# A list scheduler's other timing model in a one-core decoder trunk

## The chip, the cores and the metric

The program runs on one NeuronCore of a Trainium2 chip. The metric is the device time of one execution in microseconds (us). PE is TensorE, DVE is VectorE, ACT is ScalarE, POOL is GpSimd, SP is SyncE; SPq is SP's queue of transfers.

## The reference

One inference step of a two-layer decoder for two groups that share weights: 1024 prompt tokens and 8 x 4 sample tokens, width 1024, float32.

```python
for layer in range(DEPTH):                      # 2: layer 0 pooling, layer 1 attention
    u = _rmsnorm(x, g[0])
    if layer < N_A_LAYERS:
        mix = _pool_mix(u, buf, start_pos, w_pool[layer], pool_scale[layer])
    else:
        kv = _rmsnorm(x, kv_norm_gain) @ w_kv   # rotated keys, values, shared
        mix = _dilated_mixer(u, pos, k_all, v_all, cache_k.shape[1], w_q[b], w_o[b])
    x = x + _rmsnorm(mix, g[1])
    h = _rmsnorm(x, g[2])
    ff = jnp.square(jax.nn.relu(h @ w_up[layer])) @ w_down[layer]
    x = x + _rmsnorm(ff, g[3])
```

The pooling mixer takes trailing means over 2, 4, 8 and 16 positions per channel group, minus the token, through a 256 x 256 matrix each. The attention has three groups of windows (128, 512, 2048) with dilations 1, 4 and 16, 18 query heads and 6 key/value heads, joined by the softmax of their denominators. The sample tokens also read cached keys and values.

## The kernel before

Tokens are split into two halves: half 0 holds 512 prompt tokens and the 32 sample tokens (544 columns, worked on as two pieces of 272), half 1 holds the other 512. Activations lie with channels on partitions. Every large product is done in three passes so that float32 precision is kept with the faster number format: each operand is split into a high and a low part, and `mm3` (lines 76 to 78) multiplies high by high, high by low and low by high into one PSUM tile.

Weights stream from memory: `load_w` (line 93) fetches 128 x 1024 values into one of two `raw` buffers on SP's queue, ACT copies the high part (`wh`, line 82) and DVE subtracts to get the low part (`wl`, line 83). There are 300 such loads. The MLP goes through its 4096 hidden channels in eight chunks: up products, squared ReLU on ACT (lines 368 and 369), a split of the result, and down products added to `y` on DVE (line 383).

The stages follow one another like this: the pooling mixer of half 0 and the first chunk of its MLP; the mixer of half 1; the other chunks of the MLP of half 0; its tail beside the MLP of half 1; projections, attention blocks and the joining of half 0, with the MLP of half 1 beside them; the tail of that MLP (lines 483 to 486 are the residual) and the projections of half 1 (lines 554, 563, 600 to 625), with the output projection of half 0 and its MLP in layer 1 beside them; attention of half 1; its output projection; the last MLPs and the end.

Two things set the order of the work. The first is the program order: generators yield the time that their matmuls are thought to take, and `drive` weaves a main stream and a stream beside it by these figures and by the gaps that the main stream announces. The second is a list scheduler, which runs when the `with tile.TileContext(...)` block closes. It plays the program through a timing model of the engines, and whenever an engine is free in that model it takes, of the instructions whose operands the model says are ready, the one that stands first. What stands first is program order, except that `tc.high_priority()` moves work forward: without limit inside `first()`, by 300 places in `load_w`. The queue that each engine gets in this way is fixed in the program: on the chip an engine's instructions are issued in that order, and each waits for its semaphores. Which of a pool's buffers a tile gets is settled in the same pass.

## Time and profile before

| | us |
|---|---|
| median of 3 runs | 2099.57 |
| lowest and highest | 2098.55, 2101.83 |
| profiled execution, its own time | 2098.92 |
| span of its trace | 2097.1 |
| PE busy in it | 2000.3 |
| DVE, ACT, POOL busy | 1211.7, 932.6, 147.5 |

The span runs from the first to the last instruction of the trace; the execution's time has 1.8 us around it. Busy time of PE is that of its matmuls, which overlap, and the ends of matmuls are modelled; weight loads (PEld) overlap them.

### The profile page before, as it was taken

What the parts mean: (1) busy time and instruction counts of PE and PEld (TensorE: products, weight loads), DVE (VectorE), ACT (ScalarE), POOL (GpSimd) and SP (SyncE); (2) the same over time, 40 slices, a digit from 0 to 9 for tenths busy, and PEclk for the clock granted to TensorE, in tenths of its full rate; (3) what the DMA queues carried; (4) which work ended last, traced back from release to release, by engine and by line L of the source; (5) the groups of instructions that cost most, each with busy time, mean ns of one, the idle gap of its engine ahead of it and who ended that gap; (6) DMA issues with size and microseconds to landing.
All of it is one profiled execution on the core that took longest, in us unless ns stands there. A gap on an engine that the chain in (4) does not pass through costs nothing. (4 is left out here: it accounts for less than half of the span.)

```text
span 2097.1 us, 30907 instructions
## 1 busy us (share of the span) xinstructions
PE 2000.3 (95%) x12161; PEld 1767.9 (84%) x12161; DVE 1211.7 (58%) x2044; ACT 932.6 (44%) x1730; POOL 147.5 (7%) x146
## 2 busy tenths in 40 slices
PE   5889999999999999999998889999999999999996
PEld 4859999998889877677796779999999897888886
DVE  6668443447766665454688746555564387444446
ACT  4536333335344365353554425555553364333333
POOL 1000000000322000000014200000000003000001
PEclk8999999999999999999999999999999999999998
DMA  9213323224455654533536565452232364323331
GB/s 176 94 33 126 94 84 91 88 84 134 142 152 162 177 175 123 178 102 110 175 121 200 154 173 168 128 143 90 91 116 91 95 210 165 107 92 98 93 100 61
DMA packets 127506, 262.07 MB, mean 125 GB/s; under 512 B 34560, under 2 KB 60032, under 8 KB 126336
## 3 DMA queue, kind: packets, MB, share of 16 engines
q1 hardware_dynamic: 117504, 242.30, 39.4%
q10 hardware_dynamic: 8736, 10.78, 1.6%
q0 software_dynamic: 1120, 7.00, 1.0%
q8 instruction: 96, 1.57, 0.3%
q14 instruction: 50, 0.41, 0.1%
HBM read 218.49 MB, written 41.55 MB: 124 GB/s over the span
## 5 line engine op out<-in xcount | busy, mean ns | idle before, releaser
L76 PE MATMUL mm<-xh,wh 128*128 128x272 f32 (+1 forms) x2088 | 679.3, 327 | 21.7 <-ACT xh L345 7.0
L78 PE MATMUL mm<-xh,wl 128*128 128x272 f32 (+1 forms) x2088 | 678.4, 325 | 1.3 <-DVE wl L83 1.3
L77 PE MATMUL mm<-xl,wh 128*128 128x272 f32 (+1 forms) x2088 | 676.5, 324 | 0.7 <-DVE xl L969 0.7
L82 ACT ACTIVATE wh<-raw 128x1024 fp32r<-128x1024 f32 x300 | 317.7, 1059 | 672.8 <-PE mm L77 585.4
L83 DVE TENSOR_TENSOR wl<-raw,wh 128x1024 fp32r<-128x1024 f32 x300 | 371.9, 1240 | 331.6 <-ACT wh L82 319.6
L76 PE MATMUL mm<-h,wh 128*128 128x272 f32 (+1 forms) x1504 | 485.3, 325 | 4.4 <-ACT wh L82 2.9
L77 PE MATMUL mm<-h,wh 128*128 128x272 f32 (+1 forms) x1504 | 483.8, 323 | 1.9 <-DVE h L83 1.8
L78 PE MATMUL mm<-h,wl 128*128 128x272 f32 (+1 forms) x1504 | 481.7, 322 | 2.2 <-DVE wl L83 2.2
L76 PEld LDWEIGHTS mm<-xh,wh 128*128 128x128 f32 x2088 | 394.7, 190 | 55.8 <-ACT xh L345 7.5
L78 PEld LDWEIGHTS mm<-xh,wl 128*128 128x128 f32 x2088 | 395.6, 190 | 31.3 <-DVE wl L83 1.9
L77 PEld LDWEIGHTS mm<-xl,wh 128*128 128x128 f32 x2088 | 396.0, 190 | 30.0 <-DVE xl L969 1.2
L76 PEld LDWEIGHTS mm<-h,wh 128*128 128x128 f32 x1504 | 282.0, 188 | 31.5 <-ACT h L82 6.8
L77 PEld LDWEIGHTS mm<-h,wh 128*128 128x128 f32 x1504 | 283.6, 189 | 24.9 <-DVE h L83 5.6
L383 DVE TENSOR_TENSOR y<-mm,y 128x272 f32<-128x272 f32 (+2 forms) x344 | 176.7, 514 | 219.7 <-PE mm L78 218.9
L78 PEld LDWEIGHTS mm<-h,wl 128*128 128x128 f32 x1504 | 282.7, 188 | 22.6 <-DVE wl L83 2.9
L83 DVE TENSOR_TENSOR h<-r,h 128x272 fp32r<-128x272 f32 (+1 forms) x192 | 102.8, 538 | 104.6 <-ACT h L82 104.0
L368 ACT ACTIVATE r<-mm 128x272 f32<-128x272 f32 (+1 forms) x192 | 86.3, 452 | 75.1 <-PE mm L78 73.8
L743 ACT ACTIVATE P<-P,nm 128x256 f32<-128x256 f32 (+1 forms) x144 | 66.0, 459 | 73.8 <-DVE nm L741 66.1
L82 ACT ACTIVATE h<-r 128x272 fp32r<-128x272 f32 (+1 forms) x192 | 94.6, 496 | 6.0 <-DVE br L605 1.7
L369 ACT ACTIVATE r<-r 128x272 f32<-128x272 f32 (+1 forms) x192 | 94.6, 496 | 4.7 <-ACT r L368 0.3
L97 POOL TENSOR_TENSOR raw<-raw,gn 128x768 f32<-128x768 f32 (+2 forms) x54 | 77.3, 1448 | 154.9 <-DMA raw<-in_wqkv 108.9
L166 ACT ACTIVATE t<-y 128x544 f32<-128x544 f32 (+2 forms) x75 | 44.5, 606 | 40.0 <-DVE y L383 31.3
(249 smaller groups left out, 1625.0 us busy)
## 6 DMA issues: line engine op xcount, KB each, us to landing
raw<-in_wmlp SPq DMA_DIRECT2D x256, 512.0 KB, 3.5
raw<-in_wqkv SPq DMA_DIRECT2D x30, 512.0 KB, 3.9
raw<-in_wo SPq DMA_DIRECT2D x18, 512.0 KB, 3.5
xh<-kd SPq DMA_DIRECT2D x12, 512.0 KB, 10.5
qd<-P SPq DMA_DIRECT2D x72, 64.0 KB, 2.6
xh<-qd SPq DMA_DIRECT2D x6, 768.0 KB, 5.7
oscr<-og ACTq DMA_DIRECT2D x24, 192.0 KB, 4.0
kv<-in_vc SPq DMA_DIRECT2D x18, 256.0 KB, 4.4
```

The lines of the kernel that those rows point to most:

```text
L76: nc.tensor.matmul(out=ps, lhsT=w[0][:, c], rhs=a, start=first, stop=False)
L77: nc.tensor.matmul(out=ps, lhsT=w[0][:, c], rhs=b, start=False, stop=False)
L78: nc.tensor.matmul(out=ps, lhsT=w[1][:, c], rhs=a, start=False, stop=last)
L82: nc.scalar.activation(out=hi, in_=src, func=AF.Copy)
L83: (eng or nc.vector).tensor_tensor(out=lo, in0=src, in1=wf(hi), op=OP.subtract)
L97: nc.gpsimd.tensor_tensor(out=v, in0=v, in1=self.gn[:, g * 8:g * 8 + 8].unsqueeze(2).to_broadcast([128, 8, c1 - c0]), op=OP.mult)
L166: nc.scalar.activation(out=s, in_=src, func=AF.Square, scale=scale)
L368: nc.scalar.activation(out=r, in_=ps, func=AF.Relu)
L369: nc.scalar.activation(out=r, in_=r, func=AF.Square)
L383: nc.vector.tensor_tensor(out=ys, in0=ps, in1=ys, op=OP.add)
L743: nc.scalar.activation(out=P[:, r, z:], in_=P[:, r, z:], func=AF.Exp, bias=nm[:, r:r + 1], scale=SCL, accum_out=st[:, b, 1, kv * 3 + r:kv ...
```

## The change

The context is opened with another argument, so that the list scheduler takes its estimates of when an engine is free and when an operand is ready from the library's second timing model. The traced program, its priorities and its buffers are the same; the order inside the engines' queues and the assignment of buffers follow from the estimates.

```diff
-    with tile.TileContext(nc) as tc:
+    with tile.TileContext(nc, schedule_with_timeline_sim=True) as tc:
         build(nc, tc, h)
```

## Rows read from the trace of the kernel before

**Rows 1.** The page's first part: busy us, share of the span, instructions.
```profile
PE 2000.3 (95%) x12161; PEld 1767.9 (84%) x12161; DVE 1211.7 (58%) x2044; ACT 932.6 (44%) x1730; POOL 147.5 (7%) x146
```

**Rows 2.** Busy us by stage; then granted clock, DMA share, GB/s.
```profile
0.00:200.00 200.00, 160.39 (x927) 134.34 (x928) 141.35 (x219) 96.77 (x177) 5.35 (x6) 0.93 0.49 103
200.00:500.00 300.00, 300.00 (x2359) 297.96 (x2358) 133.06 (x213) 117.41 (x207) 3.08 (x2) 1.00 0.31 98
500.00:640.00 140.00, 135.79 (x776) 118.39 (x775) 101.50 (x150) 62.48 (x108) 38.32 (x38) 1.00 0.46 138
640.00:1040.00 400.00, 397.80 (x1969) 315.49 (x1968) 231.28 (x502) 189.52 (x421) 24.01 (x42) 1.00 0.49 149
1040.00:1300.00 260.00, 227.25 (x1371) 202.31 (x1370) 181.43 (x256) 113.38 (x199) 48.51 (x37) 0.95 0.57 167
1300.00:1650.00 350.00, 349.21 (x2635) 338.11 (x2634) 187.65 (x394) 174.41 (x361) 0.00 (x0) 1.00 0.36 110
1650.00:1750.00 100.00, 98.91 (x603) 88.41 (x602) 70.20 (x103) 59.13 (x98) 3.45 (x2) 1.00 0.46 153
1750.00:2050.00 300.00, 300.00 (x1308) 244.32 (x1307) 135.45 (x147) 104.89 (x135) 15.10 (x8) 1.00 0.36 112
2050.00:2097.00 47.00, 30.98 (x228) 28.54 (x226) 29.78 (x65) 14.56 (x31) 9.66 (x11) 0.86 0.15 51
```

**Rows 3.** PE's waits over the whole span: us in total, times, longest.
```profile
PE mm L287 <- DVE pd L274: 21.8, 7, 9.4
PE sum L184 <- ACT t L175: 8.2, 1, 8.2
PE mm L76 <- ACT xh L345: 7.0, 1, 7.0
...
PE mm L563 <- DVE ar L601: 4.6, 1, 4.6
PE mm L76 <- DVE r L554: 4.0, 1, 4.0
PE mm L76 <- ACT t L166: 3.9, 1, 3.9
```

**Rows 4.** PE in order of time at 66 us and at 1800 us.
```profile
66.09 1.50 PE L76 MATMUL mm<-xh,wh 128*128 128x272 f32 x5 [7.05 <-ACT xh L345]
67.39 0.43 PE L77 MATMUL mm<-xl,wh 128*128 128x272 f32 x1
...
1800.01 0.39 PE L76 MATMUL mm<-h,wh 128*128 128x512 f32 x1
1800.23 0.39 PE L77 MATMUL mm<-h,wh 128*128 128x512 f32 x1
1800.46 0.39 PE L78 MATMUL mm<-h,wl 128*128 128x512 f32 x1
```

**Rows 5.** Wait of SP's queue over the span; then the page's two weight-split groups.
```profile
SPq L93 <- DVE wl L83: 978.4, 206, 20.9
...
L82 ACT ACTIVATE wh<-raw 128x1024 fp32r<-128x1024 f32 x300 | 317.7, 1059 | 672.8 <-PE mm L77 585.4
L83 DVE TENSOR_TENSOR wl<-raw,wh 128x1024 fp32r<-128x1024 f32 x300 | 371.9, 1240 | 331.6 <-ACT wh L82 319.6
```

**Rows 6.** The stage from 1040 to 1300 in three parts, columns as in rows 2.
```profile
1040.00:1130.00 90.00, 83.15 (x528) 75.75 (x527) 69.68 (x87) 45.42 (x72) 19.75 (x15) 0.96 0.44 140
1130.00:1170.00 40.00, 26.85 (x100) 20.39 (x98) 38.63 (x47) 16.21 (x23) 13.02 (x8) 0.83 0.67 214
1170.00:1300.00 130.00, 117.25 (x745) 106.17 (x746) 73.12 (x124) 51.74 (x104) 15.73 (x14) 0.97 0.63 171
```

**Rows 7.** SP's issues, ACT's wait, and the chain around 1208 to 1222 us.
```profile
1208.83 0.35 SPq L93 DMA_DIRECT2D raw<-in_wmlp  x1
...
1212.12 0.42 SPq L625 DMA_DIRECT2D kd<-PTl  x1
...
1214.04 1.06 ACT L82 ACTIVATE wh<-raw 128x1024 fp32r<-128x1024 f32 x1 [6.29 <-DMA kd<-PTl]
...
1212.12 1.93 DMA kd<-PTl
1216.27 0.69 DVE PTl L83
1217.81 0.43 PE mm L77
1221.21 0.23 PE mm L77
1217.10 0.71 PE L76 MATMUL mm<-xh,wh 128*128 128x512 f32 x1 [2.91 <-DVE PTl L83]
```

## The prediction, made before the changed kernel was run

> **What bounds the kernel now.** I read the page's summary first, then the table of busy time by stage, then TensorE's waits, and only then single instructions. TensorE (PE) is busy 2000.3 us of a span of 2097.1 us [rows 1]. The reader is to see that 96.8 us are left, the gap in PE work. No change of order adds or removes a matmul, so whatever the change does to the time it does to those 96.8 us, or to the clock at which matmuls run next to a gap.
>
> The table by stage says where the gap lies [rows 2]. The first 200 us hold 39.6 us of it (200 minus 160.39), the last 47 us hold 16.0 us, and the 260 us from 1040 to 1300 hold 32.75 us. Everything else, 1590 us, holds 8.3 us: 4.2 in 500 to 640, 2.2 in 640 to 1040, 0.8 in 1300 to 1650, 1.1 in 1650 to 1750, none in the rest. So over three quarters of the run PE has work behind it whatever the other engines do, and an order that is a little better or worse there is not seen.
>
> PE's waits name the pieces [rows 3]. The 8.2 us wait is the first load and its squares, the 21.8 us are the pooling mixer waiting for VectorE (DVE), the 7.0 us are the first layer's residual. The waits of 4.6, 4.0 and 3.9 us and most of the smaller ones lie between 1040 and 1300, where three things meet: the tail of the first MLP's second half, the second half's Q/K/V projections, and the output projection of the first half with the MLP behind it.
>
> **The change part by part.** Nothing is added or removed; per matmul, split and transfer the prices stay. What moves is the order within each engine's queue, and the buffer that each tile gets, wherever two instructions were ready close together. That such choices exist is to be read from PE itself. In a steady stage the three products of a k block stand strictly one after the other, L76, L77, L78, at 0.23 us from start to start [rows 4]. At 66.09 us, where the operands arrive one by one, five L76 stand in front and the triples are broken up [rows 4]. There the estimate of ready times wrote the queue; in the steady stage program order did.
>
> *Steady stages, 200 to 500 and 1300 to 2050.* They cost nothing in either direction so long as weights come early. The cover: the queue of weight loads waits 978.4 us in all for the split that frees its buffer [rows 5], so loads stand ready and wait, not PE. If that cover went, one late split is 1.24 us of DVE and 1.06 us of ScalarE (ACT) in front of PE, and there are 300 of them in the kernel [rows 5]. I take nothing for it and keep the loss as a rival.
>
> *First 200 us.* The 8.2 us wait for the first data, and the 21.8 us behind a DVE that is the busiest engine of the mixer, are chains with one order each; I take nothing here. Both sides: at best DVE hands the first pooled tile over without the samples' work in between, at worst one more such wait of 9.4 us, the longest of the seven [rows 3].
>
> *The end.* The 16.0 us behind the last matmul are DVE and transfers in a line. Nothing.
>
> *1040 to 1300.* This is where the change can pay. Split the 32.75 us by who is busy [rows 6]. From 1130 to 1170 PE idles 13.15 us of 40, and DVE is busy 38.63 us of those 40: that part is DVE's own work, and a new order can only say which piece is late. In the other 220 us, PE idles 6.85 and 12.75 us, 19.6 in all, while DVE is busy 142.8 us (65%) and ACT 97.2 us (44%). PE stands there while both of its suppliers have time: somebody waits in line behind something that is not ready.
>
> One of them can be followed [rows 7]. From 1208.83 us SyncE issues a weight load, then seven transfers of rotated queries and keys to memory, in 3.71 us. The last of them lands at 1214.05. By the profile only then does ACT split the next weight (1.05 us, after a wait of 6.29), only after that DVE splits the transposed values (0.69 us), and PE resumes at 1217.10 after 2.91 us. The restart is paid too: the next matmuls of 512 columns come every 0.43 us, later every 0.23, the two levels 1.2 and 2.4 GHz of the granted clock. From 1217.10 to 1220.75 there are 8 of them, 3.65 us instead of 1.84: the stall costs 2.9 + 1.8 = 4.7 us.
>
> A rule of the Trainium skill stands against expecting anything of the order of transfers: "DMA: Bandwidth & Descriptors", section "Issuing engines are not separate DMA queues", says the time to initiate a DMA is usually small relative to the DMA itself. This row differs: eight issues fill 3.71 us while the last one lands 1.93 us after its issue begins. By the rule this stall would not move with the order, and with half of its 4.7 us taken out of the sum below the time would be 2094; by the row, 3.7 us of the chain are the queue's, and the sum stays.
>
> The sum. Of the 19.6 us that are neither DVE's nor the loads' own, I take half as recovered, 9.8 us: the bounds are none and all, and no row says which estimate comes nearer to the chip. One restart that goes with them gives 1.8 us. Against it I set new waits elsewhere: the stretches between 500 and 1040 and between 1300 and 1750 have 8.3 us of waiting under the present order, and I let a new order add half of that, 4.1 us. Net 9.8 + 1.8 - 4.1 = 7.5 us. The profiled execution took 2098.92 us, 0.65 us under the median of the three runs, and 2098.9 - 7.5 gives 2091 us.
>
> The bounds come from one comparison. The tail and the projections of the first half are the same code; the stretch where they start, 500 to 640, has 4.2 us of gap and the one after it 2.2 in 400 us [rows 2], while the second half's stretch has 32.75. If the second came out like the first's 4.2, 28.5 us go, and some three restarts of 1.8 with them: 34 us, 2065. If the first came out like the second, 28.5 us and three restarts come on top: 2133.
>
> **The rivals.**
> *Nothing to measure.* The new estimate moves instructions only where PE is covered, or what it wins in one queue it loses in the next. For it: 91% of the gap (88.4 of 96.8 us) lies in three stretches, and in two of them the order has little to say. Against it: in the third PE, DVE and ACT all idle together. Time 2099, within 4 us.
>
> *Slower: the hand-over of the first half loses its cover.* From 500 to 640 the same parts meet as from 1040 to 1300, and there PE idles only 4.2 us although DVE is busy 101.5 of 140. One place decides: the row of DVE work behind the first half's residual and normalization. If weight splits of 1.24 us are put ahead of the residual, PE has neither projections nor MLP to do. Half of the comparison above, 14 us, and one restart: 2115. It takes over once the new wait there exceeds what 1040 to 1300 gives back, 11.6 us. For it: the present queues leave almost no wait in that stage, so any new order is likelier to add than to remove. Against it: PE's queue takes up other work where the estimate sees a wait coming.
>
> *Slower: late weights in the steady stages.* If the new order puts splits so late that PE waits for one weight in five, 60 of 300, by 0.5 us each, less than half of a split, that is 30 us: 2129. Against it stand the 978.4 us in which loads wait for buffers.
>
> *Much faster: the order sets the rate of matmuls too.* If a new order ran the long products closer together, weight loads would be the floor: from 1750 to 2050 they are busy 244.3 of 300 us, so 56 us would go there alone, 2043. Against it: in that stretch PE is busy all 300 us and stands in strict triples already, 1308 matmuls at 0.23 us, so there is nothing to move closer [rows 2, 4]. The Trainium skill, "Perfetto Trace Analysis", section "Identifying the Most-Contended Engine", does hold that matmul busy share is a poor measure of headroom and that the busy share of weight loads (here 84%) is the one to use; the rows of this stretch do not bear that out.
>
> **How the numbers follow.** Forecast (part of 1040 to 1300 recovered): 0.41, 2091, its own range 2078 (all of the 19.6 us, one restart, no new wait) to 2095. Nothing to measure: 0.26, 2099. Hand-over of the first half: 0.23, 2115. Late weights: 0.08, 2129. Rate of matmuls: 0.02, 2043. About 0.2% (4.2 us) is what a measurement of this kernel can tell from no change, and the three runs themselves lie 3.3 us apart. So faster 0.43, same 0.26, slower 0.31. The range, 2072 to 2122, leaves out a recovery larger than my forecast's own (0.04), the rate (0.02), the upper end of the hand-over (0.07, up to the bound of 2133) and most of late weights (0.06).
>
> **What would show it.** Right: matmul count and PE busy time unchanged within a few us, 1040 to 1300 with 20 us of gap instead of 32.75, ACT's wait for the transfer before the weight split gone or short, the clock row there nearer to full, and 500 to 640 still under 6 us. Wrong: a gap that opens in 500 to 640 or between 640 and 1040; a new wait of PE on a weight split in the steady stages; the first mixer's 21.8 us changed by more than 5; or the same total with the gap in another place. The prediction also fails if PE's busy time itself moves by over 5 us, since I hold the rate of matmuls for independent of their order.

## The result, and the profile after

The changed kernel takes 2115.85 us, the median of four runs (2115.55 to 2116.64), beside 2100.7 us of the kernel before on the same chip: 1.0074 times the time, 95% interval 1.0058 to 1.0089. It is slower by 0.74%. The profiled execution took 2116.1 us, its span is 2114.2 us.

The page's first part of the changed kernel, against [rows 1]:

```profile
PE 1996.3 (94%) x12161; PEld 1779.7 (84%) x12161; DVE 1196.6 (57%) x2044; ACT 934.4 (44%) x1730; POOL 156.8 (7%) x146
```

The instructions are the same in number. PE is busy 4.0 us less, and the gap in its work is 117.9 us (2114.2 minus 1996.3) instead of 96.8. So 21.1 us more of gap, less 4.0 us of busy time, make the 17.1 us by which the span grew.

Its busy time by stage, columns as in [rows 2]:

```profile
0.00:200.00 200.00, 148.25 (x860) 125.82 (x861) 128.84 (x197) 95.53 (x172) 4.10 (x6) 0.88 0.53 100
200.00:500.00 300.00, 299.59 (x2384) 299.15 (x2383) 140.32 (x227) 118.79 (x208) 3.08 (x2) 1.00 0.30 91
500.00:640.00 140.00, 129.12 (x685) 110.02 (x684) 89.76 (x134) 59.14 (x98) 39.90 (x34) 0.95 0.46 142
640.00:1040.00 400.00, 398.14 (x2027) 323.44 (x2026) 221.84 (x496) 184.27 (x406) 23.10 (x34) 1.00 0.48 144
1040.00:1300.00 260.00, 229.21 (x1325) 203.59 (x1324) 188.38 (x275) 115.16 (x203) 58.93 (x49) 0.91 0.58 175
1300.00:1650.00 350.00, 350.00 (x2698) 342.98 (x2697) 188.28 (x403) 177.34 (x375) 0.00 (x0) 1.00 0.37 111
...
1750.00:2050.00 300.00, 297.96 (x1301) 244.75 (x1300) 140.50 (x156) 107.42 (x140) 17.79 (x10) 0.99 0.35 109
2050.00:2114.00 64.00, 43.99 (x285) 39.39 (x283) 35.96 (x70) 21.74 (x41) 9.88 (x11) 0.85 0.19 66
```

The gap grew in the first 200 us (51.75 us, was 39.6), from 500 to 640 (10.9, was 4.2) and at the end (20.0 in 64 us, was 16.0 in 47). From 1040 to 1300 it hardly moved: 30.8, was 32.75. The steady stages stay full.

PE's waits over the whole span, against [rows 3]:

```profile
PE mm L287 <- DVE pd L274: 29.9, 4, 19.1
PE mm L76 <- ACT xh L345: 10.8, 1, 10.8
PE sum L184 <- ACT t L175: 8.2, 1, 8.2
...
PE mm L76 <- DVE ar L601: 5.2, 2, 4.4
PE PT L947 <- DVE Z L83: 4.9, 1, 4.9
PE mm L76 <- DVE br L601: 4.8, 1, 4.8
PE mm L78 <- DVE wl L83: 4.7, 4, 2.0
...
PE aux L139 <- ACT t L82: 4.1, 1, 4.1
```

The wait for the first data is the same 8.2 us. The mixers' waits rose from 21.8 to 29.9 us, the longest from 9.4 to 19.1; the wait for the first split of the first half's update rose from 7.0 to 10.8. Waits for a late weight are 4.7 us in the whole program, so late weights are not what happened.

Absolute windows compare different work once one kernel lags, so I matched the two traces by work: the time at which TensorE has put the same number of columns through, minus that of the kernel before. Within a stage this lag also moves with which work is taken first, since narrow products take longer per column (in the kernel before, from 1300 to 2050 us, 0.109 us from start to start for 128 columns and 0.227 for 512); read it where a stage is over. Worked out from the matmuls of both traces, in us:

```
time in the kernel before     84    205    492    593   1005   1115   1313   1640   2048   2084
lag of the changed kernel   10.4    9.4    8.6   19.4   16.8   31.0   15.5   13.6   13.1   15.8
```

So 8.6 us were lost before the steady stretch, 10.8 between 492 and 593 (the first half's hand-over), 2.7 at the end, and from 593 to 2048 the new order won 6.3 us. The last 1.3 us of the span's 17.1 lie behind the start of the last matmul. Each lag here comes from one execution of each kernel.

**Where the first 10 us went.** First TensorE of the changed kernel, the three long waits up to 80 us, then VectorE in order of time:

```profile
37.36 5.42 PE L287 MATMUL mm<-pd,wu 128*128 128x272 f32 x16 [19.14 <-DVE pd L274]
72.76 1.50 PE L76 MATMUL mm<-xh,wh 128*128 128x272 f32 x5 [10.80 <-ACT xh L345]
77.06 0.59 PE L77 MATMUL mm<-xl,wh 128*128 128x272 f32 x1 [2.80 <-DVE xl L346]
```

```profile
25.01 3.40 DVE L233 SCALAR_TENSOR_TENSOR xh<-x0a,gn,rs 128x512 f32<-128x512 f32 x5
...
36.09 1.21 DVE L274 SCALAR_TENSOR_TENSOR pd<-s,xh 128x1024 f32<-128x1024 f32 x1
...
65.29 0.73 DVE L158 SCALAR_TENSOR_TENSOR acc<-t 128x544 f32<-128x544 f32 x1
66.05 5.17 DVE L317 TENSOR_TENSOR mixa<-mixa,acc 128x544 f32<-128x544 f32 x8
```

And VectorE of the kernel before, the same operations:

```profile
25.88 1.22 DVE L274 SCALAR_TENSOR_TENSOR pd<-s,xh 128x1024 f32<-128x1024 f32 x1
...
62.44 0.72 DVE L158 SCALAR_TENSOR_TENSOR acc<-t 128x544 f32<-128x544 f32 x1
63.20 1.36 DVE L317 TENSOR_TENSOR mixa<-mixa,acc 128x544 f32<-128x544 f32 x2
64.47 1.35 DVE L318 TENSOR_TENSOR x0a<-x0a,mixa 128x544 f32<-128x544 f32 x2
```

The reader is to see one pattern. The kernel before takes one tile through its chain: two multiplications of line 317, the two additions of line 318 that need them, and so on. The changed kernel puts all eight independent multiplications first, and in the mixer five more normalizations of line 233 ahead of the first window. The engine is as busy, but its first finished tile comes later: the first pooled tile starts at 36.09 us instead of 25.88. Most of that is made up (the update's factor, line 158, is 2.85 us later), then the update adds its own delay, and TensorE's first MLP product starts at 72.76 instead of 66.09 [rows 4].

**The hand-over.** VectorE of the changed kernel between 520 and 566 us, and then of the kernel before between 505 and 545:

```profile
522.30 5.66 DVE L483 SCALAR_TENSOR_TENSOR y<-y,gn,acc 128x544 f32<-128x544 f32 x8
527.87 1.99 DVE L484 TENSOR_TENSOR y<-y,h 128x544 f32<-128x544 f32 x3
...
558.40 0.72 DVE L83 TENSOR_TENSOR t<-rs,t 128x544 fp32r<-128x544 f32 x1
563.80 1.92 DVE L83 TENSOR_TENSOR wl<-raw,wh 128x1024 fp32r<-128x1024 f32 x1 [4.67 <-PE mm L77]
565.64 0.43 DVE L142 TENSOR_SCALAR t<-aux 128x272 f32<-128x272 f32 x1
```

```profile
505.98 0.79 DVE L483 SCALAR_TENSOR_TENSOR y<-y,gn,acc 128x544 f32<-128x544 f32 x1
...
507.81 0.72 DVE L484 TENSOR_TENSOR y<-y,h 128x544 f32<-128x544 f32 x1
...
542.87 0.72 DVE L83 TENSOR_TENSOR t<-rs,t 128x544 fp32r<-128x544 f32 x1 [0.72 <-ACT t L82]
544.08 0.44 DVE L142 TENSOR_SCALAR t<-aux 128x272 f32<-128x272 f32 x1 [0.49 <-PE aux L140]
```

The same pattern in the residual: eight of line 483, then line 484. A second thing is added: from the split of the summed squares to line 142, which takes the sum from TensorE, 7.2 us pass instead of 1.2. Two queues share this. The product that completes the sum (line 140) stands further back in TensorE's queue: it starts at 561.88, 2.8 us after the split has ended. And in VectorE's queue the low part of a weight stands ahead of line 142: it starts only at 563.80, so line 142 comes 3.5 us after that product has ended.

### The profile page after: what moved, and what is told of

Its sections match the earlier page's. It is cut to its first block, busy times and chain, and to the rows that moved or that the text cites. A ratio compares the mean times of both kernels' runs of the same rounds, so it can differ in the third digit from the quotient of the medians.

```text
span 2114.2 us, 30980 instructions
## 1 busy us (share of the span) xinstructions
PE 1996.3 (94%) x12161; PEld 1779.7 (84%) x12161; DVE 1196.6 (57%) x2044; ACT 934.4 (44%) x1730; POOL 156.8 (7%) x146
## 5 line engine op out<-in xcount | busy, mean ns | idle before, releaser
L76 PE MATMUL mm<-xh,wh 128*128 128x272 f32 (+1 forms) x2088 | 683.0, 329 | 30.0 <-ACT xh L345 10.8
L77 PE MATMUL mm<-h,wh 128*128 128x272 f32 (+1 forms) x1504 | 479.6, 322 | 0.0
L76 PE MATMUL mm<-h,wh 128*128 128x272 f32 (+1 forms) x1504 | 474.9, 324 | 0.4 <-DVE y L383 0.3
L383 DVE TENSOR_TENSOR y<-mm,y 128x272 f32<-128x272 f32 (+2 forms) x344 | 172.3, 513 | 205.1 <-PE mm L78 204.5
L97 POOL TENSOR_TENSOR raw<-raw,gn 128x768 f32<-128x768 f32 (+2 forms) x54 | 83.6, 1567 | 181.1 <-DMA raw<-in_wqkv 98.9
L287 PE MATMUL mm<-pd,wu 128*128 128x272 f32 (+1 forms) x96 | 36.1, 529 | 29.9 <-DVE pd L274 29.9
```

Of the source, the lines that this page charges most:

```text
L76: nc.tensor.matmul(out=ps, lhsT=w[0][:, c], rhs=a, start=first, stop=False)
L77: nc.tensor.matmul(out=ps, lhsT=w[0][:, c], rhs=b, start=False, stop=False)
L97: nc.gpsimd.tensor_tensor(out=v, in0=v, in1=self.gn[:, g * 8:g * 8 + 8].unsqueeze(2).to_broadcast([128, 8, c1 - c0]), op=OP.mult)
L287: nc.tensor.matmul(out=ps, lhsT=wu[g // 2][:, c:c + 128], rhs=pd[:, ki, o:o + wd], start=ki == 0, stop=ki == 1)
L383: nc.vector.tensor_tensor(out=ys, in0=ps, in1=ys, op=OP.add)
```

## The experiments

Theory: the order in the queues explains all of it, at a few places, each with its price; the order that finishes no tile before all are begun is what costs. Rivals: the buffers that the tiles got; a mismatch between queues rather than one queue's order; gains in one place that are taken back in the next.

The order can be forced without a wait: an edge without a semaphore between neighbours of one queue only tells the scheduler which comes first. `ORDER` holds instruction names, queue by queue, as another kernel has them; the runs differ in the opening of the context and in this list alone, which the diffs below give in words. The edit, for a base with the other model:

```diff
-    with tile.TileContext(nc) as tc:
+    with tile.TileContext(nc, schedule_with_timeline_sim=True) as tc:
         build(nc, tc, h)
+        queue_order(nc, tc)
...
+def queue_order(nc, tc):
+    made = {i.name: i for i in nc.cur_bb.bb.instructions}
+    kind = mybir.DependencyInfo(mybir.DependencyClass.NoSync, mybir.DependencyReason.DATA)
...
+        if last is not None:
+            tc.add_manual_dep(made[name], last, kind, reason="queue order")
+        last = name
```

The edges bind only the queues and the stretch that are named; the scheduler writes everything else anew around them. In the traces of the runs on the kernel before, TensorE, VectorE and ScalarE have its order again by 215 us at the latest, but the runs that bind the head or the hand-over of the changed kernel differ from it in other places too, up to 1080 to 1230 us. And where one queue is bound, the others move with it. So the price of a place includes what the scheduler did in answer.

Instruction numbers below are those of the traced program: 0 to 983 is the first half's mixer and update with its first MLP chunk ("the head"), 984 to 1499 the second half's mixer and update, 4880 to 5759 the first half's hand-over. The lag of each profiled run behind the kernel before, as above:

```
time in the kernel before              84    165    205    492    593   1005   1313   2048
changed kernel                       10.4   10.4    9.4    8.6   19.4   16.8   15.5   13.1
... all queues old                    1.0    1.1    1.1    1.1    1.0    3.1    5.2    4.7
... VectorE's queue old               0.3    2.1   12.3   11.6   21.3   41.0   55.7   63.9
... head old                          1.8   -8.2   -9.2  -10.0    0.1   -1.7   -4.8   -6.6
... hand-over old                    11.4    9.7    8.7    7.9    8.2    8.0    5.2    1.2
... head and hand-over old           -0.1  -11.6  -12.7  -13.4  -13.1  -12.1  -13.5  -15.8
kernel before, head new              10.0   10.9   10.9   10.9   10.7   10.7   13.1   12.7
kernel before, second mixer new       0.8   -0.7    5.9    5.9    5.6    6.2    7.3    7.0
kernel before, mixers as in the best -0.6  -12.4  -13.5  -13.5  -13.4  -13.5  -14.3  -13.9
```

**All queues of the changed kernel in the old order.**

```diff
+ORDER: all five queues, whole program, as in the kernel before
```

> The changed kernel, with every queue (PE, DVE, ACT, POOL, SyncE) held by issue-order edges to the order it has in the kernel before. Theory 'queues': the change acts through the order inside the queues alone, so this gives the time of before, 2100 us within 4. Rival 'buffers': the buffers that the second model hands out cost the time, so this stays near the changed kernel, 2112 to 2116.

Measured: 2101.09 us, 1.0005 of the kernel before (0.9994 to 1.0015). The difference is gone. In the trace TensorE, VectorE, ScalarE and the SP queue run the sequences of the kernel before (the profiled execution took 2103.58 us, 2.5 above the median, hence its lag). The order of the queues, with whatever choice of buffers goes along with it, is the whole effect; this also shows that the edges themselves cost nothing that can be measured.

**VectorE's queue alone in the old order.**

```diff
+ORDER: VectorE's queue, whole program, as in the kernel before
```

> The changed kernel, with DVE's queue alone held to the order of before; the four other queues are the scheduler's. Theory 'DVE goes breadth first': most of the 17 us comes back, 2099 to 2105. Rival 'PE's queue': the sums over channels stand too far back among PE's matmuls, and DVE's order is only a symptom; then no more than a third comes back, 2110 to 2116.

Measured: 2168.02 us, 1.0324 (1.0309 to 1.034), 52 us slower than the changed kernel. The head came back (lag 0.3 at 84 us), and then nearly every stage lost: 10 us at the second half's mixer, 10 at the hand-over, 20 from 593 to 1005. Among its waits:

```profile
PE mm L287 <- DVE pd L274: 22.4, 6, 9.4
PE mm L78 <- DVE wl L83: 17.3, 15, 3.0
```

The mixers' wait is nearly that of [rows 3], but TensorE now waits 15 times for a weight's low part. Here one queue in the old order, with the others written around it by the other model, is worse than either order as a whole. The theory that one could mend VectorE alone everywhere falls.

**The head in the old order.**

```diff
+ORDER: all five queues, instructions 0 to 983, as in the kernel before
```

> The changed kernel, with all queues held to the order of before for the program's first part only (mixer, update and first MLP chunk of half 0). Theory 'two places': matched by the amount of matmul work done, the changed kernel is 10.4 us late by 84 us of the span and stays so; all of it comes back and the rest is untouched, 2105 to 2107. Rival 'given back later': what is late there is caught up behind other stalls anyway, so less than 4 us come back, 2112 to 2116.

Measured: 2097.28 us, 0.9989 (0.9978 to 1.0001), 18.6 us less than the changed kernel and more than the head's 10.4. The lag table shows both parts: 8.6 of the expected 10.4 us at 84 us, and then 10.0 more between 84 and 165, where the queues were left free, which I had not expected.

**The hand-over in the old order.**

```diff
+ORDER: all five queues, instructions 4880 to 5759, as in the kernel before
```

> The changed kernel, with all queues held to the order of before for the hand-over of half 0 only (tail of its MLP, first chunk of the MLP of half 1, start of its projections). Theory 'two places': 10.7 us come back, the step in lag between 492 and 593 us, 2104 to 2107. Rival 'given back later': under 4 us, 2112 to 2116, since the lag shrinks and grows again by 10 us between 750 and 1300.

Measured: 2103.03 us, 1.0014 (1.0004 to 1.0023), 12.8 us less than the changed kernel. From 492 to 593 us the lag stays (7.9, then 8.2) where the changed kernel loses 10.8. This is the hand-over's price, 1 us below the range expected.

**Head and hand-over.**

```diff
+ORDER: all five queues, instructions 0 to 983 and 4880 to 5759, as in the kernel before
```

> The changed kernel with all queues in the order of the kernel before in two stretches: from the start through the first chunk of the first half's first MLP, and in the first half's hand-over from one layer to the next. Theory (each place has its own price, and nothing later depends on it): the two gains measured one at a time add, 18.6 + 12.8 = 31.4, so 2115.9 - 31.4 = 2084.5 us, 0.7% under the kernel before. Rival (what one place gives is taken back in the next stretch, since weights or the sum chains there are then waited for): no more than the better of the two, about 2097 us. In between, from 2088 to 2093, some of it is given back, and the lag behind the kernel before, measured at equal matmul work, shows where.

Measured: 2089.08 us, 0.9945 (0.9928 to 0.9962): 26.8 of the 31.4 us. The places nearly add. Of the missing 4.6 us the lag shows where most were given back: from 593 to 2048 us this run wins 2.7 us on the kernel before (-13.1 to -15.8), where the changed kernel wins 6.3 and the two single runs 6.7 and 7.0. The stages up to 1313 account for it (0.4 won, against 3.0 to 4.9 in the other three). Which wait takes it there I did not find out.

**With the end as a third stretch.**

```diff
+ORDER: all five queues, instructions 0 to 983, 4880 to 5759 and 16500 to the end, as in the kernel before
```

> As the kernel of two stretches, with a third: the last projections and sums of the program, from the last MLP chunks to the end, also in the order of the kernel before. Theory: the changed kernel fell 2.7 us further behind the kernel before in the last 60 us, so 2084.5 - 3 = about 2081 us. Rival (the lag at the end is only what a late start of the last weights does, and goes with the lag before it): the same as the kernel of two stretches, 2084 to 2085 us.

Measured: 2085.94 us, 0.993 (0.9911 to 0.9948), faster than both kernels by 0.7% and 1.4%. It is 3.1 us under the run before it, as the theory of separate places has it, but the two intervals overlap, and the total is nearer to the rival's 2084 to 2085 than to 2081 (both were counted from 2084.5, where the run before it came out at 2089.08). In the traces the run before it loses 2.7 us between 2048 us and the last matmul, and this one 0.4. The end's share is likely, not settled.

**The kernel before with the new head.**

```diff
+ORDER: all five queues, instructions 0 to 983, as in the changed kernel
```

> The kernel before, with all queues from the start through the first chunk of the first half's first MLP in the order of the changed kernel, and nothing else. Theory (the order of the first stretch costs its delay of the first product and of the update by itself): the lag at 84 us was 10.4 us, so 2099.6 + 10 = about 2110 us. Rival (the second half's mixer, still in its old order, takes up the delay, since it has waits of its own there): 2100 to 2104 us. A second rival (the old order behind it fits the new head worse): over 2114 us.

Measured: 2111.26 us, 1.0052 (1.0037 to 1.0067), 11.9 us slower. The lag is 10.0 at 84 us, 10.7 to 10.9 from 165 to 1005, and 12.7 at 2048. The new head costs this by itself, and nothing behind it takes it up.

**The kernel before with the second half's mixer in the changed order.**

```diff
+ORDER: all five queues, instructions 984 to 1499, as in the changed kernel
```

> The kernel before, with all queues of the second half's mixer and update alone in the order that the changed kernel has there. Theory (in that stretch the changed order is the better one by itself, as the run with the head in the old order showed between 126 and 182 us): 2099.6 - 13 = about 2087 us. Rival (the gain there was only made up time, in a stretch that had slack because the head had been in a different order): 2098 to 2101 us, not to be told from the kernel before.

Measured: 2105.4 us, 1.0025 (1.0014 to 1.0036): 6.0 us slower, so neither the gain nor "no difference". The 10 us that the run with the old head won here are not in the changed kernel's order of this mixer. In it TensorE waits for a weight's low part behind the update:

```profile
PE mm L78 <- DVE wl L83: 5.2, 1, 5.2
```

I had to look for another cause, and found it in TensorE's sixteen products of line 184, which sum the second half's squares. Their rows (first and last start), in the kernel before, in this run, and in the run with the old head:

```profile
L184 PE MATMUL sum<-t,ones x16: 590/592/592, 116.5 to 122.9; 128*128 128x512 f32 x16
```

```profile
L184 PE MATMUL sum<-t,ones x16: 590/592/593, 117.3 to 123.7; 128*128 128x512 f32 x16
```

```profile
L184 PE MATMUL sum<-t,ones x16: 591/592/594, 94.0 to 104.1; 128*128 128x512 f32 x16
```

Where they stand at 94 us, the second half's mixer runs on VectorE while TensorE still has the first MLP chunk; where they stand at 117 us, it begins when TensorE has run out of that chunk.

**The kernel before with both mixers as in the run of three stretches.**

```diff
+ORDER: all five queues, instructions 0 to 1999, as in the run with three stretches held
```

> The kernel before, with all queues from the start to the end of the second half's first update in the order of the kernel with three stretches: the first half's head as in the kernel before, but the second half's squares summed on TensorE at 92 to 102 us, under the first MLP chunk, instead of at 116 to 123 us behind its last product. Theory (the place of these sixteen products is what gave 13 us between 120 and 163 us, and everything behind it keeps its old order): lag of minus 10 to minus 11 us from 165 us to the end, 2089 us. Rival (the gain needs the other model's order behind it): 2095 to 2100 us.

Measured: 2088.84 us, 0.9951 (0.9938 to 0.9964), beside the 2089 expected. The lag is -12.4 at 165 us and stays between -13 and -15 to the end. The first half's head is the old one and everything behind is old too; the products of line 184 stand from 91.6 to 101.7 us. So the second half's sums and mixer, started under the first chunk, are worth 11 us with the old order behind them; with the other model's order behind them the run with the old head won 10. TensorE waits 2.7 us for `pd` between 84 and 210 us, and 8.9 in the kernel before. Yet VectorE has all eight normalizations of line 233 in a row here too (109.59 to 114.97 us): going by operation is not seen to cost anything while TensorE has other work. The place of the sixteen products and the order of the mixer behind them were moved together here; the run above, which moved the mixer's order alone, lost time.

**The breadth of the update alone.**

```diff
+ORDER: VectorE's queue, instructions 394 to 426, as in the changed kernel
```

> The kernel before, with only VectorE's sixteen operations of the first half's update (eight multiplications of line 317, eight additions of line 318, and what stands among them) in the order of the changed kernel: all multiplications ahead of the first addition. Theory (a first result is late by the independent operations put ahead of it): the first addition comes after eight multiplications instead of two, 6 x 0.65 = 3.9 us later, and nothing makes that up: 2099.6 + 4 = 2103.5 us. Rival (the additions then run at twice the density and ScalarE's splits set the pace, so TensorE's first product alone is late): under 2101.5 us.

Measured: 2107.57 us, 1.0041 (1.0028 to 1.0053), 7.7 us slower, twice what I had worked out. VectorE and TensorE's two waits up to 90 us:

```profile
61.60 0.73 DVE L157 SCALAR_TENSOR_TENSOR t<-t 128x544 f32<-128x544 f32 x1 [2.16 <-ACT t L154]
62.36 0.72 DVE L158 SCALAR_TENSOR_TENSOR acc<-t 128x544 f32<-128x544 f32 x1
63.12 5.17 DVE L317 TENSOR_TENSOR mixa<-mixa,acc 128x544 f32<-128x544 f32 x8
68.21 5.17 DVE L318 TENSOR_TENSOR x0a<-x0a,mixa 128x544 f32<-128x544 f32 x8
73.29 5.65 DVE L346 SCALAR_TENSOR_TENSOR xl<-x0a,gn,xh 128x544 fp32r<-128x544 f32 x8
```

```profile
PE mm L76 <- ACT xh L345: 10.9, 1, 10.9
PE mm L77 <- DVE xl L346: 2.8, 1, 2.8
```

The first addition is 3.74 us later than in the kernel before (68.21 against 64.47), and the first wait grows by that, from 7.0 to 10.9. What I left out is the third operation of the chain: the low parts of line 346 now stand behind all eight additions, and TensorE waits a second time, 2.8 us. Together 6.7 us, and the lag at 84 us is 8.1. TensorE's clock gives most of the rest: behind these waits 29 products of 272 columns come every 0.23 us (granted clock 0.50 from 69.8 to 79.6 us, the lower of the two levels) before they come every 0.125, against 17 in the kernel before; 12 times 0.1 is 1.2 us. So the update explains most of the changed kernel's 10.4 us in the head; its 2.85 us in the mixer are the rest. Only VectorE's order was prescribed, but the scheduler moved TensorE's and ScalarE's instructions with it between 67 and 96 us, so this is the price of the breadth with what followed from it.

**VectorE's queue alone in the old order, in the head.**

```diff
+ORDER: VectorE's queue, instructions 0 to 983, as in the kernel before
```

> The changed kernel, with VectorE's queue alone in the order of the kernel before, from the start through the first chunk of the first half's first MLP. Theory (VectorE's order is what made the head late): the 10.4 us of the head come back, 2105 us, or more with the second half's sums moved as in the run that held all queues there. Rival (TensorE's and ScalarE's queues, left to the other model, stand out of step with it, as with VectorE held through the whole program): 2116 us or later.

Measured: 2096.89 us, 0.9988 (0.9979 to 0.9997), the same as with all five queues held there. In the head VectorE's order is the cause: the scheduler fits the other queues to it.

**VectorE's queue alone in the old order, in the hand-over.**

```diff
+ORDER: VectorE's queue, instructions 4880 to 5759, as in the kernel before
```

> The changed kernel, with VectorE's queue alone in the order of the kernel before, in the first half's hand-over from one layer to the next. Theory (VectorE's order of the residual is what is late there): most of the 12.8 us that all queues gave, 2104 to 2107 us. Rival (the products that sum the squares stand late in TensorE's queue, whatever VectorE does): at most 4 us of it, 2112 us or later.

Measured: 2112.08 us, 1.0066 (1.0053 to 1.008): 3.8 of the 12.8 us. The theory falls here, and the rival's number fits. The interval overlaps that of the changed kernel, and 2.2 of the 3.8 us stand in the lag at 492 us already (6.4 against 8.6), ahead of the first instruction in another order, so little of it can be the hand-over's.

**TensorE's queue alone, and TensorE's with VectorE's, in the hand-over.**

```diff
+ORDER: TensorE's queue, instructions 4880 to 5759, as in the kernel before
...
+ORDER: TensorE's and VectorE's queues, instructions 4880 to 5759, as in the kernel before
```

> The changed kernel, with TensorE's queue alone in the order of the kernel before, in the first half's hand-over. Theory A (the sum products of lines 139 and 140 stand too far back in TensorE's queue, and VectorE waits for them): about 9 of the 12.8 us, 2107 us. Theory B (the gain needs both queues in one order): under 4 us of it, 2112 us or later, as with VectorE's alone. Theory C (a queue held alone is out of step with the others, as over the whole program): over 2117 us.

> The changed kernel, with TensorE's and VectorE's queues in the order of the kernel before, in the first half's hand-over, and ScalarE's, GpSimd's and the DMA queues left to the other model. Theories A and B: the 12.8 us of all queues, 2103 us. Rival (ScalarE's splits and squares, or the DMA queues, carry a part): 2106 to 2112 us.

Measured: TensorE's alone 2116.35 us, 1.0069 (1.0053 to 1.0084), which gives nothing; both 2106.05 us, 1.0024 (1.0014 to 1.0034), 9.8 of the 12.8 us. Theory B holds: it needs both queues in one order. The time lies at the edge of the second rival's range and not at 2103, so the remaining 3.0 us may lie in ScalarE's and the DMA queues; but the intervals of this run and of the one with all five overlap, so that share is not settled. Line 142 on VectorE, which takes the sum, with VectorE's queue old, with TensorE's old, and with both:

```profile
559.08 0.44 DVE L142 TENSOR_SCALAR t<-aux 128x272 f32<-128x272 f32 x1 [0.48 <-PE aux L140]
```

```profile
559.93 0.44 DVE L142 TENSOR_SCALAR t<-aux 128x272 f32<-128x272 f32 x1 [4.59 <-PE aux L140]
```

```profile
552.88 0.44 DVE L142 TENSOR_SCALAR t<-aux 128x272 f32<-128x272 f32 x1 [0.49 <-PE aux L140]
```

Against 565.64 in the changed kernel the first two are each about 6 us earlier and the third 12.8: this chain adds up. With one queue alone the time does not follow, since TensorE then stands in front of other operands (3.7 us for `y` of line 381 and 3.4 for `h` with its own queue old, 3.7 for the squares of line 166 with VectorE's).

## Why the prediction was wrong

**The step that failed** is "First 200 us ... are chains with one order each; I take nothing here". VectorE's row there is not one chain but eight tiles with three or four operations each, and the scheduler may go by tile or by operation. It went by operation, and the head was 10.4 us late. My upper bound for this step, one more wait of 9.4 us, was nearly the size; I gave it no chance. It was also the sign I named for being wrong: the mixers' 21.8 us moved by 8.1. [rows 4] had shown the order at 66 us on TensorE only. The row that would have told me, VectorE's own order at 63 us, pairs of line 317 and line 318, I had not read.

**A second term was mis-sized.** By the lag the change lost 8.6 us up to 492, 10.8 in the hand-over, 2.7 and 1.3 at the end, and won 6.3 between. My sum had nothing for the first, 4.1 for all new waits of 500 to 1040 and 1300 to 1750 together, nothing for the end, and 11.6 won. With the head at nothing the kernel would still be 8.5 us slower, so the 4.1, a half of the present waits with no row behind it, failed as well: one place cost more than twice that.

**The rival that came true** is the hand-over of the first half, at 2115 us; the time is 2115.85. It came true in place and size there (10.8 us of lag, 12.8 by the run, against 14 and a restart of 1.8) but only in part by the mechanism I named. A weight split does stand ahead of the residual's sum in VectorE's queue, at 563.80 us, and holds line 142 back by 3.5 us; the residual's own operations in breadth and the sum product in TensorE's queue make the rest, and I had named neither. And the total agrees in part by chance: I had the head at nothing and the later stages unchanged in that case, where they are +8.6 and -6.3.

**1040 to 1300.** I took 9.8 us of waiting and 1.8 of restart as won there. The stall that I followed [rows 7] is gone: in the changed trace TensorE has no wait for `PTl` in this stage. But new waits stand there (5.8 us for a transfer of keys, 5.2 and 4.8 for line 601, 4.9 for line 83, 4.7 for line 1000), and from 1005 to 1313 the lag falls by only 1.3 us. The gap there is 30.8 us, not 20.

I had also read that stall wrongly. The row names a transfer as what ended ScalarE's wait, but the weight split reads nothing of that transfer and started at 1214.04 us, before the 1214.05 that I took for its landing. What ended just before is one of TensorE's products with the high part of a weight, at 1213.95:

```profile
1213.56 0.39 PE L77 MATMUL mm<-xl,wh 128*128 128x512 f32 x1
```

So by these times ScalarE waited for TensorE to be done with a weight buffer, and TensorE then stood still because in VectorE's queue a weight's low part (1215.12 us, 1.23 long) was ahead of `PTl`. The order of VectorE's queue was the point, and not 3.7 us of issues; setting eight issues against one transfer was no fair comparison either, since in that row one issue takes 0.42 us and its transfer 1.93. No run moved this stall alone.

**The net of the stages behind the first hand-over**, from 593 to 2048, is 6.3 us won. That this is near the 7.5 of my whole sum is chance: 7.5 was 11.6 won in one stage less 4.1 lost in others, and the 6.3 came as 2.6 up to 1005 us, 1.3 up to 1313 and 2.4 behind it.

**The end** cost 2.7 us where I took nothing. **Late weights** did not come: 4.7 us of such waits, and the loads wait longer for a buffer than before, against [rows 5]:

```profile
SPq L93 <- DVE wl L83: 1052.0, 206, 33.1
```

**PE's busy time** moved by 4.0 us, under the 5 I had set. But over all the runs it goes from 1990.4 us (hand-over old) to 2021.8 (VectorE's queue old), so it is not independent of the order; what moves it I did not settle. The Trainium skill, "Perfetto Trace Analysis", section "Identifying the Most-Contended Engine", would read TensorE's headroom from the weight loads' busy share and the arithmetic done, and not from the matmuls' busy share. These runs cannot tell the two shares apart: with three stretches held, in the kernel before, in the changed one and with VectorE's queue old the weight loads are busy 85.2, 84.3, 84.2 and 82.4% of the span, and the matmuls 95.9, 95.4, 94.4 and 93.3%; both go with the time.

**What stays open.** Why the second model sorts by operation cannot be read from a trace. I suppose that it decides on an instruction before it knows its operand to be near, so that a dependent one counts as not ready and the next independent one goes ahead. This is argued, not shown.

## What to carry to other kernels

When a scheduler's estimate changes, look at the rows where one engine feeds an idle TensorE tile by tile (a norm, a residual, a split), and ask for each whether the queue goes by tile or by operation: its busy time says nothing of that, the start of the first finished tile says more. Price the whole chain up to the last operand that the first product needs, not its first link only. And hold or move queues together: a good order of one engine against the others' was worth nothing to 3.8 us in the hand-over, hardly more than the scatter, where two together gave 9.8, and over the whole program it cost 52 us.

## What the runs showed of the hardware

A dependent VectorE operation behind the one that it needs costs little here. Line 158 starts 0.76 us after line 157, on which it depends (62.36 and 61.60 in the run with the update in breadth). Eight independent operations of the same kind and width (line 483 of the changed kernel) take 5.66 us, 0.71 each. So, as an estimate from these two rows, going by operation saves some 0.05 us for each pair, and it delays the first finished tile by whole operations. And starting one mixer's sums 25 us earlier (91.6 against 116.5), with the mixer's order that went with it and under matmuls that were there anyway, was worth 11 us, while the whole change moved the time by 15.
